# A list scheduler given deadlines and measured durations, and a last norm that VectorE scales out of PSUM

## The chip, the cores and the metric

One NeuronCore of a Trainium2 chip runs the whole program. The metric is the device time of one execution in microseconds. Three executions of the kernel before were timed: 2470.39, 2470.67 and 2472.54 us, so its median is 2470.67 us. A fourth, profiled execution took 2468.28 us; all rows below come from that one.

## The reference, cut to what matters

A trunk of two layers works on x, 1024 tokens by 1024 channels, in float32. Each layer has a token mixer and a gated ConvFFN, and a final RMSNorm closes the trunk.

```python
for i in range(DEPTH):                     # DEPTH = 2
    h = rms_norm(x, norm_g[i, 0]) * (1.0 + sc1) + sh1
    y = spatial_gating_mixer(h, ...) if i % 2 == 0 else hgrn2_mixer(h, ...)
    x = x + g1 * y
    h = rms_norm(x, norm_g[i, 1]) * (1.0 + sc2) + sh2
    x = x + g2 * conv_ffn(h, ...)          # (gelu(conv(gate)) * conv(val)) @ w_down
return rms_norm(x, final_g)                # x * rsqrt(mean(x*x) + eps) * g
```

The shifts, scales and gates sh, sc, g are six slices of `silu(c) @ ada_w[i] + ada_b[i]`. The first mixer (gMLP) projects to 4096 columns, normalises half of them, mixes tokens in blocks of 128 per head and multiplies by the other half. The second (HGRN2) is a gated linear recurrence with eight heads, chunked along the tokens.

## The kernel before, in words

The residual x lives in SBUF transposed, as the tile `xT`: 128 partitions, 8 channel groups d, 1024 tokens, worked on in two halves of 512. Each large product is made on TensorE from operands that are split into a high and a low part: three matmuls (high by high, high by low, low by high) are summed in one PSUM bank by `mm3` (L247). So every weight and every activation needs a split ahead of its matmuls: ScalarE makes the high part (L445), and VectorE or GpSimd the low part by a subtraction (L448; `n`, `w`, `h` and `raw` are the buffers that it writes). The large products are further done two blocks at a time with seven partial products for eight (`Pairs`), which costs VectorE sums of operands (`p_comb`, L455) and, out of PSUM, ScalarE copies (`snap`, L673) and VectorE sums of the results (`add`, L676).

The norms: ScalarE squares a piece (L399), the squares are summed over the eight groups by VectorE (L404), TensorE sums over partitions (L308), a chain of ten small VectorE instructions takes the reciprocal root (L281 to L291), VectorE writes it to a diagonal (L313), TensorE broadcasts it to all partitions (L318), and ScalarE copies it from PSUM to SBUF (L322). Then x is scaled (L970 in the first norm, L1667 in the last) and, before a mixer, split again by `p_h` (ScalarE L432, VectorE L433). The conditioning is made on VectorE by dot products with ada_w, one pair of 128x1024 operands each (`p_dot`, L255); there are 81 of them, spread over the first layer's work.

No engine's order is written out by hand. The kernel records some 8,300 operations in a class `Plan` as (engine, duration, function, predecessors, hand-given priority, port), where predecessors follow from the parts of tiles read and written. `emit` (L162 to L203) then plays them through a list scheduler: at each step it takes the ready operation that could start earliest on its engine by the durations given, and at equal starts the one with the lower hand-given number. Operations marked `port` (most VectorE work with two SBUF inputs, and GpSimd's) exclude each other in that plan. The instructions are issued on each engine in the order of the planned starts, and on the chip each engine runs them in that order, waiting for semaphores.

Places named later: `done` (L1210) multiplies the two halves of the gMLP in SBUF and PSUM; `entry` (L1228) scales a piece of x for the gMLP's second projection; `shifted` (L621) makes an operand of the seven products; `p_evac` (L387) adds a finished PSUM bank to `xT`; `lv_mm`, `adv` and `adv_t` (L1462 to L1490) are the recurrence's levels. At the end, `f1_last` takes the last two quarters of 256 tokens: groups d = 4 to 7 of both are done earlier, and d = 0 to 3 come last. `p_final` (L1667) scales `xT` by the broadcast root and issues a store (L1669) at once; the final gain is put on ahead of it by ScalarE (`p_gain`, L1674).

Of the kernel before, what the change touches and what calls it, by code (L numbers as in the profile page):

```python
# [98 lines left out]

class Plan:  # L100
# [9 lines left out]
    LOAD = 2.0  # L110

# [50 lines left out]
    def emit(self):  # L162
        n = len(self.ops)
        left = [0] * n
        users = [[] for _ in range(n)]
        for i, o in enumerate(self.ops):
            for q in set(o[3]):
                users[q].append(i)
                left[i] += 1
# [7 lines left out]
        while len(order) < n:  # L177
            best = None
            for eng, lst in ready.items():
                f = free.get(eng, 0.0)  # L180
                for i in lst:
                    o = self.ops[i]
# [4 lines left out]
            eng, dur, fn, _, _, pt = self.ops[i]  # L187
# [6 lines left out]
            for u in users[i]:  # L194
                e2 = self.ops[u][0]
                lat = self.LOAD if eng == "D" else self.LAT if e2 != eng else self.CHAIN if eng == "V" else 0.0
                est[u] = max(est[u], end[i] + lat)
                left[u] -= 1
                if not left[u]:
                    ready.setdefault(e2, []).append(u)  # L200
        for _, _, i in sorted(order):
            self.ops[i][2]()
        return max(end)  # L203
# [10 lines left out]
def trunk(tc, a, pool, psum, dram):  # L214
# [168 lines left out]
    def p_evac(pl, ps, d, hs, gate, which, pr):  # L383
# [5 lines left out]
        return pl.op("V", 0.15 + 0.6 * w, fn, r=(ps, x, modrg(*which, d)), w=(x,), pr=pr)  # L389

    def p_sum(pl, nm, d, accv, sqs, pr, eng="V", first=0):
# [15 lines left out]
    def p_stats(pl, nm, accv, ps, rbv, pr, part=0):  # L407
# [8 lines left out]
        pl.op("V", 1.3, chain, r=(ps,), w=(sm,), pr=pr)  # L416
# [4 lines left out]
    def p_t(pl, nm, l, sub, d, tv, rbv, pr):  # L421
        i = (l * 2 + sub) * KT + d
        return pl.op("V", 0.67, lambda: V.scalar_tensor_tensor(out=tv.f, in0=xT[:, d, nm.hs],
# [18 lines left out]
    def p_split(pl, src, hi, lo, eng, pr, *preds):  # L442
# [4 lines left out]
        return pl.op(eng, (0.1 + 0.53 * w) if eng == "V" else 0.1 + 1.17 * w,  # L447
# [131 lines left out]
    class Pairs:  # L579
# [32 lines left out]
        def combos(self, k, pr, t1=None):  # L612
# [7 lines left out]
            def shifted(out, x, s, y, srg, pr):  # L620
                pl.op("V", 0.67, lambda: V.scalar_tensor_tensor(out=out.f, in0=x.f, scalar=s, in1=y.f,  # L621
# [26 lines left out]
        def pair(self, j, fine=False):  # L648
# [26 lines left out]
            def add(c, ps, i):  # L675
                pl.op("V", 0.75, lambda: V.tensor_tensor(out=c.f, in0=ps.f, in1=c.f, op=ALU.add), r=(ps, c),  # L676
# [1112 lines left out]
```

## Time and profile before

| | |
|---|---|
| timed executions (us) | 2470.39, 2470.67, 2472.54 |
| profiled execution (us) | 2468.28 |
| span of its profile (us) | 2466.5 |
| PE busy | 2419.2 us, 98% of the span |
| DVE busy | 1992.3 us, 81% |
| ACT busy | 1205.9 us, 49% |
| POOL busy | 487.2 us, 20% |
| mean granted TensorE clock | 0.993 |

The profiled execution has 1.78 us outside its span and lies 2.39 us under the median. PE is TensorE's matmuls, DVE is VectorE, ACT is ScalarE, POOL is GpSimd, SP the engine that issues the transfers. The rows of the trace further down have the source line behind an L; a tile's buffer number is left out of its name, so `w<-w,w` reads two buffers of one family and writes a third.

### The profile page before, as it was taken

What the parts mean: (1) busy time and instruction counts of PE and PEld (TensorE: products, weight loads), DVE (VectorE), ACT (ScalarE), POOL (GpSimd) and SP (SyncE); (2) the same over time, 40 slices, a digit from 0 to 9 for tenths busy, and PEclk for the clock granted to TensorE, in tenths of its full rate; (3) what the DMA queues carried; (4) which work ended last, traced back from release to release, by engine and by line L of the source; (5) the groups of instructions that cost most, each with busy time, mean ns of one, the idle gap of its engine ahead of it and who ended that gap; (6) DMA issues with size and microseconds to landing.
All of it is one profiled execution on the core that took longest, in us unless ns stands there. A gap on an engine that the chain in (4) does not pass through costs nothing.

```text
span 2466.5 us, 33569 instructions
## 1 busy us (share of the span) xinstructions
PE 2419.2 (98%) x11850; PEld 2024.6 (82%) x11850; DVE 1992.3 (81%) x3179; ACT 1205.9 (49%) x2067; POOL 487.2 (20%) x294
## 2 busy tenths in 40 slices
PE   9999999999999999999999999999999999999997
PEld 7878777788788888888899898888777888888886
DVE  8989987988998888967746666658998998889766
ACT  5324654455555554445544444435454555554544
POOL 0232211122222221013321111100312222220122
PEclk9999999999999999999999999999999999999998
DMA  9997678621333324734110111123302332238332
GB/s 356 305 344 272 200 238 295 222 77 39 116 102 108 116 94 143 262 112 120 51 48 35 58 42 56 44 73 106 106 24 95 98 132 99 94 127 283 95 116 81
DMA packets 156411, 332.00 MB, mean 135 GB/s; under 512 B 15825, under 2 KB 34641, under 8 KB 156242
## 3 DMA queue, kind: packets, MB, share of 16 engines
q1 hardware_dynamic: 156242, 329.86, 40.0%
q8 instruction: 93, 1.52, 0.3%
q14 instruction: 76, 0.62, 0.1%
HBM read 254.82 MB, written 74.97 MB: 134 GB/s over the span
## 4 chain that ended last, share of the span: by engine, by line
PE 76%; DVE 8%; DMA 3%; ACT 2%; issue 1%; SPq 0%; DVEq 0%; ACTq 0%
PE pb L247 69%; PE pb L1462 3%; DMA n<-in_wo 1%; DMA xT<-vd 1%; DMA n<-in_down 1%; DVE h L448 1%; ACT xT L1171 1%; PE pb L1531 1%; PE pb L1551 1%; DVE w L448 1%; DVE raw L831 1%; PE pb L1553 1%; DVE n L448 0%; DVE xT L455 0%; DVE w L455 0%
## 5 line engine op out<-in xcount | busy, mean ns | idle before, releaser
L247 PE MATMUL pb<-h,w 128*128 128x512 f32 (+1 forms) x4212 | 981.7, 389 | 12.8 <-DVE h L448 4.1
L247 PE MATMUL pb<-n,w 128*128 128x512 f32 x3936 | 951.6, 394 | 6.8 <-ACT wk L673 4.4
L247 PEld LDWEIGHTS pb<-h,w 128*128 128x128 f32 x4212 | 785.5, 188 | 185.0 <-DVE h L448 9.6
L247 PEld LDWEIGHTS pb<-n,w 128*128 128x128 f32 x3936 | 731.9, 188 | 160.0 <-ACT wk L673 5.5
L448 POOL TENSOR_TENSOR w<-w,w 128x512 fp32r<-128x512 f32 x158 | 252.2, 1604 | 862.5 <-ACT w L445 784.2
L445 ACT ACTIVATE w<-w 128x512 fp32r<-128x512 f32 x384 | 237.3, 626 | 212.4 <-PE pb L247 121.7
L247 PE MATMUL pb<-w,n 128*128 128x512 f32 (+1 forms) x1536 | 273.6, 338 | 3.0 <-POOL w L448 1.7
L247 PEld LDWEIGHTS pb<-w,n 128*128 128x128 f32 x1536 | 237.9, 190 | 36.3 <-POOL w L448 2.1
L831 DVE SCALAR_TENSOR_TENSOR raw<-wk,prm,raw 128x1024 f32<-128x1024 f32 x168 | 251.7, 1520 | 16.2 <-ACT raw L827 14.1
L448 POOL TENSOR_TENSOR w<-raw,w 128x1024 fp32r<-128x1024 f32 (+1 forms) x48 | 118.3, 2473 | 536.0 <-ACT w L445 467.0
L448 DVE TENSOR_TENSOR w<-w,w 128x512 fp32r<-128x512 f32 x226 | 166.4, 741 | 41.5 <-ACT w L445 41.4
L673 ACT ACTIVATE wk<-pb 128x512 f32<-128x512 f32 x160 | 95.2, 599 | 174.5 <-PE pb L247 161.9
L445 ACT ACTIVATE w<-n 128x512 fp32r<-128x512 f32 x136 | 85.7, 630 | 158.0 <-PE pb L247 143.7
L676 DVE TENSOR_TENSOR wk<-pb,wk 128x512 f32<-128x512 f32 x160 | 109.2, 687 | 50.1 <-PE pb L247 30.9
L448 DVE TENSOR_TENSOR w<-n,w 128x512 fp32r<-128x512 f32 x136 | 103.4, 763 | 56.5 <-ACT w L445 56.4
L445 ACT ACTIVATE h<-h 128x512 fp32r<-128x512 f32 x198 | 122.3, 619 | 40.8 <-DMA h<-gact 23.5
L827 ACT ACTIVATE raw<-wk,prm 128x1024 f32<-128x1024 f32 x84 | 104.2, 1243 | 41.6 <-DVE wk L676 34.9
L448 POOL TENSOR_TENSOR h<-h,h 128x512 fp32r<-128x512 f32 x48 | 67.8, 1413 | 258.8 <-ACT h L445 247.4
L1468 DVE TENSOR_TENSOR wk<-wk 128x256 f32<-128x256 f32 x192 | 95.6, 523 | 23.7 <-PE pb L1462 11.0
L255 DVE SCALAR_TENSOR_TENSOR h<-h,raw 128x1024 f32<-128x1024 f32 x81 | 111.1, 1404 | 3.5 <-DMA h<-in_ada 3.4
L448 DVE TENSOR_TENSOR h<-h,h 128x512 fp32r<-128x512 f32 x150 | 102.1, 686 | 8.7 <-ACT h L445 8.7
L1472 ACT ACTIVATE wk<-wk 128x256 f32<-128x256 f32 x192 | 73.9, 415 | 59.4 <-PE pb L1462 44.2
(217 smaller groups left out, 2431.8 us busy)
## 6 DMA issues: line engine op xcount, KB each, us to landing
w<-in_up SPq DMA_DIRECT2D x88, 512.0 KB, 3.5
h<-in_ada SPq DMA_DIRECT2D x81, 512.0 KB, 6.3
act<-raw SPq DMA_DIRECT2D x154, 256.0 KB, 2.0
h<-act SPq DMA_DIRECT2D x124, 256.0 KB, 2.7
n<-in_down SPq DMA_DIRECT2D x64, 256.0 KB, 5.3
h<-gact SPq DMA_DIRECT2D x56, 256.0 KB, 2.7
gact<-xT SPq DMA_DIRECT2D x52, 256.0 KB, 3.9
vd<-h SPq DMA_DIRECT2D x32, 256.0 KB, 5.1
```

The source lines that it names most:

```text
L247: PE.matmul(ps, L[i // 2], R[i % 2], start=first and i == 0 and not more, stop=last and i == 2, skip_group_check=more)
L255: V.scalar_tensor_tensor(out=raw, in0=raw, scalar=1.0, in1=condr, op0=ALU.mult, op1=ALU.mult, accum_out=mod[:, m:m + 1])
L445: pl.op("S", 0.2 + 0.43 * w, lambda: S.activation(hi.r, src.f, AF.Copy), r=(src,), w=(hi,), pr=pr)
L448: lambda: e.tensor_tensor(out=lo.r, in0=src.f, in1=hi.f, op=ALU.subtract), *preds,
L673: pl.op("S", 0.6, lambda: S.activation(c.f, ps.f, AF.Copy), r=(ps,), w=(c,), pr=p(i) - 10)
L676: pl.op("V", 0.75, lambda: V.tensor_tensor(out=c.f, in0=ps.f, in1=c.f, op=ALU.add), r=(ps, c), w=(c,), pr=p(i) - 8)
L827: pl.op("S", 1.15, lambda: S.activation(y.f, wk[:, o + PADW:o + PADW + T], AF.Identity, bias=pc("conv_b", l * NUP + b), scale=cw(2)), r=(c ...
L831: pl.op("V", 1.17, lambda w=w: V.scalar_tensor_tensor(out=y.f, in0=wk[:, o + w:o + w + T], scalar=cw(w), in1=y.f, op0=ALU.mult, op1=ALU.ad ...
L1171: S.activation(x, x, AF.Identity, scale=lnr[:, tb:tb + 1], bias=nmr[:, tb:tb + 1])
L1462: PE.matmul(ps_()[0:m, c, :], K.f[:, c * P:c * P + m], q, start=True, stop=True)
L1468: V.tensor_tensor(out=halves_(X2, s)[:, :, i, :], in0=halves_(X, s)[:, :, i, :], in1=pair2()[:, :, o].unsqueeze(2).to_broadcast([P, 256 // ...
L1472: S.activation(halves_(X2, s)[:, :, i, :], halves_(X, s)[:, :, i, :], AF.Copy)
```

## The change

It has two parts. First, the planner runs twice. Its first pass goes by the hand-given numbers as before; TensorE's order is taken from it. From that order, with the durations given, each operation gets a latest start: the position in time of the TensorE work that needs it, less the durations and lags in between. The second pass is the same list scheduler, with these latest starts in the place of the hand-given numbers (for TensorE its position in the first pass; for what no TensorE work needs, the end of all TensorE work). Some thirty durations given to `pl.op` are replaced by others that stand nearer to the rows of the trace.

Second, the last norm: in `f1_last` the squares of the last pieces are no longer added up by VectorE but summed by TensorE in PSUM (`p_root`), the broadcast root stays in PSUM, and VectorE scales from there; GpSimd keeps five pieces of the first quarter, three of them held until the second chain of small instructions is through, and scales them by a copy that ScalarE makes. Stores are separate operations (`p_store`), six instead of fifteen.

```diff
+    def schedule(self, users, rank):
...
-                    t = max(f, est[i], port if o[5] else 0.0)
-                    if best is None or (t, o[4], i) < best:
-                        best = (t, o[4], i)
+                    t = max(f, est[i], port if self.ops[i][5] else 0.0)
+                    if best is None or (t, rank[i], i) < best:
+                        best = (t, rank[i], i)
...
+    def emit(self):
...
+        order = self.schedule(users, [o[4] for o in self.ops])
+        for _ in range(self.ROUNDS):
+            on_pe = [i for i in order if self.ops[i][0] == "PE"]
+            late, t = [FAR] * n, 0.0
+            for i in on_pe:
+                late[i] = t
+                t += self.ops[i][1]
+            for i in reversed(order):
+                for u in users[i]:
+                    late[i] = min(late[i], late[u] - self.lag(i, u) - self.ops[i][1])
+            rank = [min(x, t) for x in late]
+            for k, i in enumerate(on_pe):
+                rank[i] = k
+            order = self.schedule(users, rank)
+        for i in order:
             self.ops[i][2]()
...
-        pl.op("V", 1.3, chain, r=(ps,), w=(sm,), pr=pr)
+        pl.op("V", 1.95, chain, r=(ps,), w=(sm,), pr=pr)
...
-        return pl.op(eng, (0.1 + 0.53 * w) if eng == "V" else 0.1 + 1.17 * w,
+        return pl.op(eng, (0.11 + 0.57 * w) if eng == "V" else 0.1 + 1.22 * w,
...
-        pl.op("V", 2.2, fn, r=(kv(96 * hf, 96),), w=((f"small{hf}", 0, 16), kv(3264 + 8 * hf, 8), kv(3280 + 4 * hf, 4),
+        pl.op("V", 3.3, fn, r=(kv(96 * hf, 96),), w=((f"small{hf}", 0, 16), kv(3264 + 8 * hf, 8), kv(3280 + 4 * hf, 4),
...
+    def p_root(nm, sums, ps, pr, part):
+        c_, sm, accv = nm.n // P, (f"small{part}", 0, 16), sums[0]
+        nm.acc = accv.f
+        for i, x in enumerate(sums):
+            def fn(i=i, x=x):
+                for c in range(c_):
+                    PE.matmul(ps.f[:, c:c + 1], x.f[:, c * P:(c + 1) * P], ones[:, 0:1], start=i == 0 and c == 0,
+                              stop=i == len(sums) - 1, skip_group_check=True)
+            pl.op("PE", 0.23 * c_, fn, r=(x,), w=(ps,), pr=pr)
...
     def f1_last(mm, at):
...
+        _, b0 = p_root(nms[1], (accv[1], tails[3]), bv(4), at() - 4, 0)
+        for d in range(4):
             piece(1, d)
+        pl.op("S", 0.4, lambda: nms[1].copy_rb(bank[4][:, 0:256], rbv[1].f), b0, w=(rbv[1],), pr=at() - 4)
+        for d in (7, 0):
+            p_final(nms[1], d, 1, rbv[1], "G", at() - 3, b0)
+        for d in (4, 5):
+            p_final(nms[1], d, 1, bv(4, 0, 256), "V", at() - 2, b0)
+        p_store(nms[1], 4, 2, at())
+        c1, b1 = p_root(nms[2], (accv[2], *(tails[4 + d] for d in range(4))), bv(5), at() - 4, 1)
+        for d in (1, 2, 3):
+            p_final(nms[1], d, 1, rbv[1], "G", at(), b0, c1)
+        p_final(nms[1], 6, 1, bv(4, 0, 256), "V", at() - 1, b0, c1)
+        p_store(nms[1], 6, 2, at())
+        for d in range(0, KT, 2):
+            p_final(nms[2], d, 2, bv(5, 0, 256), "V", at() + 1, b1)
```

All lines of the file behind `emit` stand 25 lines lower after the change (L448 is L473 there, L455 is L480, L1210 is L1235, L1228 is L1253, L255 is L280, L433 is L458, L970 is L995, L387 is L412).

At three places VectorE's order is shown as it stands before and after. The first is the start, from the second dot product to the first low half. `h11` is the first norm's scratch, `n100` the low half of the first piece of the activations, `w1`, `w3` and `w5` low halves of weights. Before:

```order
L970 SCALAR_TENSOR_TENSOR h11_186<-xT_64,amul_71,pb6_81 128x512
L448 TENSOR_TENSOR w1_196<-h2_133,w0_167 128x1024
L448 TENSOR_TENSOR w3_202<-h3_145,w2_176 128x1024
L433 SCALAR_TENSOR_TENSOR n100_207<-h11_186,mod_70,n000_200 128x512
L255 SCALAR_TENSOR_TENSOR h4_162,mod_70<-h4_162,raw2_67 128x1024
L255 SCALAR_TENSOR_TENSOR h5_172,mod_70<-h5_172,raw2_67 128x1024
L263 TENSOR_TENSOR mod_70<-mod_70,prm_63 128x2
L267 SCALAR_TENSOR_TENSOR amul_71<-mod_70,prm_63 128x1
L970 SCALAR_TENSOR_TENSOR h11_186<-xT_64,amul_71,h10_198 128x512
```

After:

```order
L995 SCALAR_TENSOR_TENSOR h11_187<-xT_64,amul_71,pb6_81 128x512
L473 TENSOR_TENSOR w3_199<-h3_133,w2_165 128x1024
L473 TENSOR_TENSOR w1_204<-h2_141,w0_175 128x1024
L280 SCALAR_TENSOR_TENSOR h4_161,mod_70<-h4_161,raw2_67 128x1024
L280 SCALAR_TENSOR_TENSOR h5_171,mod_70<-h5_171,raw2_67 128x1024
L288 TENSOR_TENSOR mod_70<-mod_70,prm_63 128x2
L292 SCALAR_TENSOR_TENSOR amul_71<-mod_70,prm_63 128x1
L995 SCALAR_TENSOR_TENSOR h11_187<-xT_64,amul_71,h10_206 128x512
L458 SCALAR_TENSOR_TENSOR n100_208<-h11_187,mod_70,n000_202 128x512
```

The low half `n100` moved from ahead of the next two dot products and the second piece's scaling to behind them.

The second place is in the gMLP, where two `done` products (`xT<-pb5`) release the next spatial mixing on TensorE. Before:

```order
L448 TENSOR_TENSOR w3_1389<-w10_1550,w3_1389 128x512
L1228 SCALAR_TENSOR_TENSOR raw0_65<-raw0_65,amul_71,h10_198 128x512 x2
L1228 SCALAR_TENSOR_TENSOR raw1_66<-raw1_66,amul_71,h10_198 128x512
L1199 SCALAR_TENSOR_TENSOR pb5_80<-pb5_80,prm_63,wk_68 128x512
L1199 SCALAR_TENSOR_TENSOR pb4_79<-pb4_79,prm_63,wk_68 128x512
...
L455 TENSOR_TENSOR xT_64<-raw1_66,raw0_65 128x512
L455 TENSOR_TENSOR w10_1550<-w10_1550 128x512
L621 SCALAR_TENSOR_TENSOR raw1_66<-raw1_66,small_73 128x512
L1210 TENSOR_TENSOR xT_64<-pb5_80,xT_64 128x512
```

After:

```order
L473 TENSOR_TENSOR w3_1382<-w10_1491,w3_1382 128x512
L480 TENSOR_TENSOR h4_1857<-xT_64 128x512
L1253 SCALAR_TENSOR_TENSOR raw0_65<-raw0_65,amul_71,h10_206 128x512
L1224 SCALAR_TENSOR_TENSOR pb5_80<-pb5_80,prm_63,wk_68 128x512
L1224 SCALAR_TENSOR_TENSOR pb4_79<-pb4_79,prm_63,wk_68 128x512
L1235 TENSOR_TENSOR xT_64<-pb5_80,xT_64 128x512
L1253 SCALAR_TENSOR_TENSOR raw1_66<-raw1_66,amul_71,h10_206 128x512 x2
L480 TENSOR_TENSOR xT_64<-raw1_66,raw0_65 128x512
L280 SCALAR_TENSOR_TENSOR h3_133,mod_70<-h3_133,raw2_67 128x1024
L646 SCALAR_TENSOR_TENSOR raw1_66<-raw1_66,small_73 128x512
```

Three of the four `entry` scalings, a sum of operands and a `shifted` moved from ahead of the product to behind it. Over the whole queue sixteen operations that stood ahead of it now stand behind (the others are dot products, low halves and sums further up), and none the other way.

The third place is VectorE's end. Before:

```order
L387 SCALAR_TENSOR_TENSOR xT_64<-pb3_78,mod_70,xT_64 128x256
L404 TENSOR_TENSOR h1_16829<-h1_16829,h8_16846 128x256 x2
L281 TENSOR_SCALAR small_73<-pb1_76 128x2
...
L291 SCALAR_TENSOR_TENSOR small_73<-small_73 128x2
L313 TENSOR_TENSOR h1_16829<-prm_63,small_73 128x256
L1667 TENSOR_TENSOR xT_64<-xT_64,h9_17519 128x256 x4
L1667 TENSOR_TENSOR xT_64<-xT_64,h9_17519 128x2x256
```

After:

```order
L412 SCALAR_TENSOR_TENSOR xT_64<-pb3_78,mod_70,xT_64 128x256
L1692 TENSOR_TENSOR xT_64<-xT_64,pb4_79 128x256 x2
L306 TENSOR_SCALAR small_73<-pb5_80 128x2
...
L316 SCALAR_TENSOR_TENSOR small_73<-small_73 128x2
L338 TENSOR_TENSOR h1_87<-prm_63,small_73 128x256
L1692 TENSOR_TENSOR xT_64<-xT_64,pb4_79 128x256
L1692 TENSOR_TENSOR xT_64<-xT_64,pb5_80 128x2x256 x4
```

The additions of squares (L404) are gone from ahead of the last chain, two scalings out of PSUM stand in their place, and five scalings follow it as before, of which four instead of one are twice as wide.

## Rows read from the trace of the kernel before

**Rows 1.** Busy time by stretch: start:end, length, five engines, PEclk, DMA share, GB/s.
```profile
60.00:1050.00 990.00, 972.49 (x4376) 800.45 (x4375) 881.43 (x1255) 493.72 (x821) 211.56 (x125) 1.00 0.54 183
1050.00:1700.00 650.00, 648.64 (x3908) 569.23 (x3907) 413.94 (x927) 293.79 (x586) 114.99 (x58) 1.00 0.20 64
1700.00:1900.00 200.00, 189.99 (x862) 153.62 (x861) 182.97 (x288) 103.25 (x174) 49.22 (x28) 0.98 0.25 82
1900.00:2440.00 540.00, 539.59 (x2382) 445.17 (x2381) 446.73 (x576) 277.32 (x432) 103.64 (x69) 1.00 0.40 128
2440.00:2466.50 26.50, 11.43 (x80) 10.01 (x78) 16.78 (x45) 7.36 (x18) 7.58 (x10) 0.71 0.24 80
```

**Rows 2.** What TensorE waited for, 60 to 2440 us: total us, times, longest.
```profile
PE pb L247 <- ACT wk L673: 4.8, 3, 3.8
PE pb L247 <- ACT xT L673: 4.6, 4, 1.6
...
PE pb L247 <- DVE n L448: 2.9, 1, 2.9
...
PE pb L1194 <- ACT h L445: 2.4, 1, 2.4
PE pb L247 <- ACT h L445: 2.2, 2, 2.1
PE pb L247 <- POOL w L448: 1.7, 1, 1.7
PE pb L318 <- DVE h L313: 1.6, 4, 0.4
PE pb L1524 <- DVE wk L1468: 0.9, 1, 0.9
```

**Rows 3.** Busy time by stretch, behind four of these waits; PEclk is third from last.
```profile
263.35:266.76 3.41, 3.41 (x14) 2.93 (x13) 3.41 (x7) 3.15 (x7) 0.89 (x1) 0.50 0.42 129
...
403.30:406.71 3.41, 3.41 (x8) 2.73 (x9) 3.01 (x5) 2.33 (x5) 1.29 (x1) 0.50 0.98 285
...
1874.44:1881.27 6.83, 6.19 (x15) 4.84 (x16) 3.76 (x6) 1.08 (x3) 1.27 (x1) 0.50 0.31 115
...
1739.00:1742.40 3.40, 3.40 (x15) 2.78 (x16) 3.40 (x6) 0.77 (x2) 0.00 (x0) 1.00 0.63 160
```

**Rows 4.** GpSimd's low halves, a group of the page's part 5: busy us, mean ns.
```profile
L448 POOL TENSOR_TENSOR w<-w,w 128x512 fp32r<-128x512 f32 x158 | 252.2, 1604 | 862.5 <-ACT w L445 784.2
```

**Rows 5.** Timeline of the start, 20 to 28 us: start, duration, engine, operation.
```profile
21.39 5.75 PE L247 MATMUL pb<-w,n 128*128 128x512 f32 x24 [0.93 <-ACT n L432]
22.28 0.75 DVE L433 SCALAR_TENSOR_TENSOR n<-h,mod,n 128x512 fp32r<-128x512 f32 x1
22.94 1.22 DVE L255 SCALAR_TENSOR_TENSOR h<-h,raw 128x1024 f32<-128x1024 f32 x1
...
26.41 1.22 DVE L448 TENSOR_TENSOR w<-h,w 128x1024 fp32r<-128x1024 f32 x1
...
27.31 0.98 PE L247 MATMUL pb<-w,n 128*128 128x512 f32 x3 [0.17 <-ACT n L432]
```

**Rows 6.** Timeline of the end, 2448 to 2466 us, in order of start.
```profile
2450.85 5.75 POOL L1667 TENSOR_TENSOR xT<-xT,h 128x256 f32<-128x256 f32 x8 [17.26 <-ACT h L322]
...
2451.61 12.13 SPq L1669 DMA_DIRECT2D out_y<-xT  x15
...
2453.24 0.67 DVE L282 TENSOR_SCALAR small<-small 128x2 int32<-128x2 int32 x1
...
2456.66 0.16 DVE L288 SCALAR_TENSOR_TENSOR small<-small 128x2 f32<-128x2 f32 x1
...
2459.18 0.38 ACT L322 ACTIVATE h<-pb 128x256 f32<-128x256 f32 x1 [7.16 <-PE pb L318]
2459.59 3.09 DVE L1667 TENSOR_TENSOR xT<-xT,h 128x256 f32<-128x256 f32 x5 [1.73 <-ACT h L322]
```

**Rows 7.** Transfers of 2440 to 2467 us: size of one, median us to landing.
```profile
out_y<-xT SPq DMA_DIRECT2D x14, 128.0 KB, 1.7
out_y<-xT SPq DMA_DIRECT2D x1, 256.0 KB, 2.2
```

**Rows 8.** GpSimd's timeline, 265 to 272 us.
```profile
265.88 6.83 POOL L448 TENSOR_TENSOR w<-w,w 128x512 fp32r<-128x512 f32 x2 [8.82 <-ACT w L445]
```

**Rows 9.** Busy time by stretch, as in rows 1, around the wait at 263 us.
```profile
246.00:308.00 62.00, 57.60 (x285) 48.28 (x284) 59.21 (x93) 43.25 (x93) 13.97 (x7) 0.97 0.61 200
```

More of the change, by code (lines that the diff above doesn't have):

```diff
@@ L110 @@
     LOAD = 2.0
+    ROUNDS = 1
     def __init__(self):
@@ L160, in op, with lag @@
         return i
-    def emit(self):
+    def lag(self, i, u):
+        eng, e2 = self.ops[i][0], self.ops[u][0]
+        return self.LOAD if eng == "D" else self.LAT if e2 != eng else self.CHAIN if eng == "V" else 0.0
+    def schedule(self, users, rank):
         n = len(self.ops)
[L164 to L169, printed above, removed]
+        left = [len(o[3]) for o in self.ops]
         est, end = [0.0] * n, [0.0] * n
@@ L194, in emit @@
             for u in users[i]:
-                e2 = self.ops[u][0]
-                lat = self.LOAD if eng == "D" else self.LAT if e2 != eng else self.CHAIN if eng == "V" else 0.0
-                est[u] = max(est[u], end[i] + lat)
+                est[u] = max(est[u], end[i] + self.lag(i, u))
                 left[u] -= 1
                 if not left[u]:
-                    ready.setdefault(e2, []).append(u)
-        for _, _, i in sorted(order):
+                    ready.setdefault(self.ops[u][0], []).append(u)
+        return [i for _, _, i in sorted(order)]
+    def emit(self):
+        n = len(self.ops)
+        users = [[] for _ in range(n)]
+        for i, o in enumerate(self.ops):
+            for q in o[3]:
+                users[q].append(i)
+        order = self.schedule(users, [o[4] for o in self.ops])
[13 more added lines that the diff above has]
+        for i in order:
             self.ops[i][2]()
-        return max(end)
 def trunk_body(tc, a):
@@ L1665, in p_final, with p_store @@
         xr = [xrg(d + i, nm.hs) for i in range(k)]
[L1666 to L1669 removed]
+        pl.op(eng, (0.11 + 0.57 * w) if eng == "V" else 0.1 + 1.22 * w,
+              lambda: e.tensor_tensor(out=x, in0=x, in1=rb.f[:, 0:nm.n].unsqueeze(1).to_broadcast([P, k, nm.n]), op=ALU.mult),
+              *preds, r=(*xr, *((rb,) if eng == "G" or not preds else ())), w=xr, pr=pr, port=eng == "G" or not preds)
+    def p_store(nm, d, k, pr):
+        x = xT[:, d:d + k, nm.hs]
+        pl.op("D", 0.3 + 0.73 * k * nm.n / 512, lambda: nc.sync.dma_start(a["out"][:, d:d + k, nm.hs], x),
+              r=[xrg(d + i, nm.hs) for i in range(k)], pr=pr)
     def p_gain(nm, d, pr):
@@ L1675, in p_gain, with chain @@
               w=(xr,), pr=pr)
+    def p_root(nm, sums, ps, pr, part):
[7 more added lines that the diff above has]
+            pl.op("PE", 0.23 * c_, fn, r=(x,), w=(ps,), pr=pr)
+        rt, ops = small_ops(ps.f[:, 0:c_], c_, 1.0 / D, part)
+        def chain():
+            for f in ops:
+                f()
+        last = pl.op("V", 1.95, chain, r=(ps,), w=(sm,), pr=pr)
+        pl.op("V", 0.42, lambda: nm.diag(rt), r=(sm,), w=(accv,), pr=pr)
+        return last, pl.op("PE", 0.45, lambda: nm.bcast(ps.f[:, 0:nm.n]), r=(accv,), w=(ps,), pr=pr)
     def f1_first(pr):
@@ L1691, in piece @@
         def piece(i, d):
-            p_evac(pl, mm(d, 256 * i, 256), d, nms[1 + i].hs, gate2(1), (1, 5), at() - 4)
-            summed(i, d)
-        def finish(i, engs):
-            p_stats(pl, nms[1 + i], accv[1 + i], bv(i), rbv[1 + i], at() - 4, i)
-            d = 0
-            for e in engs.split():
-                k = int(e[1:])
-                p_final(nms[1 + i], d, k, rbv[1 + i], e[0], at() + d)
-                d += k
+            nm = nms[1 + i]
+            p_evac(pl, mm(d, 256 * i, 256), d, nm.hs, gate2(1), (1, 5), at() - 4)
+            if i == 0 and d < 3:
+                summed(i, d)
+            else:
+                x, q = xrg(d, nm.hs), tails[4 * i + d]
+                pl.op("S", 0.42, lambda: S.activation(q.f, xT[:, d, nm.hs], AF.Square), r=(x,), w=(q,), pr=at() - 4)
+            p_gain(nm, d, at() - 3)
+        last = two(f1.bc[11], F32)[0].life
+        tails = {3: View(acl, 0, 256), **{4 + d: View(last, 256 * d, 256) for d in range(4)}}
         for d in range(4, KT):
```

60 lines of the change are left out of this document (27 added, 33 removed).

## The prediction

> **What bounds the kernel now.** TensorE. I read first the busy time by stretch. From 60 to 2440 us its idle time is 990 - 972.49, plus 1.36, 10.01 and 0.41, together 29.3 us [rows 1]: nearly all of it lies in the first layer up to 1050 us and in the 200 us after the recurrence, the stretches in which VectorE is busy for 89 and 91% of the time. In the recurrence and in the second ConvFFN there is next to nothing to win. Next the waits by releaser: single waits of 1 to 4 us, which end with a ScalarE copy out of PSUM (9.4 us in seven), a VectorE low half, ScalarE high halves, and one GpSimd low half [rows 2]. Behind the longest of them the clock falls: three stretches of 3.41, 3.41 and 6.83 us stand at 0.50, that is 1.2 GHz for 2.4 GHz [rows 3]. TensorE worked in them for 3.41, 3.41 and 6.19 us and did half as much as at full clock, so they cost 1.7 + 1.7 + 3.1 = 6.5 us more. The waits of mid-run are thus worth 29.3 + 6.5 = 35.8 us. The last 26.5 us hold 11.43 us of TensorE work and a serial end [rows 1].
>
> **The mid-run waits.** The new tie-break changes no amount of work, only who goes first, so I costed each wait by VectorE's queue: the operations that stand ahead of the awaited one before and behind it after, less those that go the other way, by their durations in the trace. At the gMLP's wait (263 us, 2.4 us, ended on paper by a ScalarE high half, in fact by the `done` product ahead of it in the same chain) sixteen operations or 13.3 us go out and none comes in; the excerpt shows five of them. A wait can be paid back by that much, at most by its own length, so it goes, with its clock. By the same count 5.5 us go out ahead of the 2.9 us low half at 1739 us, 18 less 7 ahead of one at 432 us, and 2 to 10 us ahead of the ScalarE copies that release the seven products: those copies are short and wait themselves for VectorE's sums in the same bank chain. At the GpSimd wait of 1.7 us (163 us) 17 us go out of the chain behind it and 1.5 come in.
>
> Four do not go. The load of `h` at 402 us (2.06 us, a transfer queued behind as many bytes as before) keeps its wait and its low clock: 2.1 + 1.7 = 3.8 us. The recurrence's wait (0.9 us) has no work moved out ahead of it; a norm's broadcast at 1811 us (0.45 us) gets 0.7 to 1.4 us more ahead of it. At 1875 us only 2.5 us go out ahead of a 3.8 us wait, so 1.3 us stay, shorter than waits that left the clock alone. Together 6.5 us stay and 29.3 us go.
>
> **New waits.** The queue says where slack went. VectorE's low halves come 3 to 8 us earlier against their matmuls nearly everywhere. GpSimd's in the first ConvFFN come later: against 12 to 13.6 us before they keep 1 to 5 us, since work of no urgency now ranks behind and the first pair's products are pulled ahead by up to 16 us. At 281 us one stands 2.9 us behind its need. GpSimd's mean is 1.60 us [rows 4], so a margin of 1 us holds if nothing stretches it. I take 3 us, that one; the bounds are 0 and 6, with one such wait more.
>
> **The start.** The excerpt puts two dot products, two small operations and a scaling ahead of the first low half `n100`. They take from 22.94 to 26.41 us, 3.47 us [rows 5]. TensorE's first eight matmuls need no low half; the other sixteen of the 24 do. Those eight last 8/24 of 5.75 = 1.9 us, to about 23.3 us, while the low half was ready at 23.03, some 0.2 us ahead. So TensorE waits 3.3 us in mid-row, and falls back 2.9 us, since the two pauses just after (0.17 us and one of 0.2) are absorbed. What cover is there? None: all other products ahead need the same half. A 2.4 us wait lowered the clock, a 2.9 us one at 1739 us didn't [rows 3]; this one is longer and comes soon after the engine's start, so I add 1.7 us: 4.6 us. Bounds: 0 (if the dots wait less, or TensorE's later slack absorbs it) and 4.6. ScalarE's first high half moves ahead of a copy, which starts TensorE some 0.6 us earlier and gains nothing for the sixteen.
>
> Here a page bears. The Trainium skill ("TensorE: Matmul & The Clock Gate", Part 1: The HAM clock gate) says that the gate's default is the throttled state and activity releases it; it speaks against every order that leaves TensorE idle early. By it the start is 4.6 us, and without it 2.9; the row at 1739 us shows an idle engine that kept its clock, so the 1.7 us are not certain.
>
> **The end.** Before, half of the last chain of small instructions ran at 0.64 to 0.67 us for 0.16 beside GpSimd's eight scalings [rows 6], 2.4 us in five. After, two GpSimd scalings are ahead of the chain and three behind it, so most of that goes; I leave 1 us of it for the two. The ScalarE copy of 0.38 us goes from the path, and one addition of squares (0.4 us) too. Against that, the stores start later: nearly all of them after the chain, 1.5 MB of 2, where before eight had already gone out beside it. Fifteen stores of 128 KB take 1.7 us each to landing, overlapped, one of 256 KB 2.2 [rows 7]; the stretch's densest part ran at 200 to 290 GB/s, so 1.5 MB need 5.2 to 7.5 us. The scalings begin about 1.9 us earlier (2459.6 to 2457.7), and 1.5 MB from there land at 2463 to 2465.5, against 2465.5. I take -0.9 us; bounds -3.5 (transfers keep up) and +1 (they don't).
>
> The scalings out of PSUM have no row. The nearest is the same operation out of SBUF, five in 3.09 us beside two of GpSimd [rows 6]. The Trainium skill ("SBUF — State Buffer", Who interferes with whom) says that a VectorE instruction with at most one SBUF input, outside the two-port modes, doesn't contend with GpSimd: by it the PSUM scalings run free, some 0.5 us better than my sum. A row goes against reading it widely: L282 has one tile as input and took 0.67 us beside GpSimd [rows 6].
>
> **The sum.** -29.3 (waits and clock) + 3 (new waits) + 4.6 (start) - 0.9 (end) = -22.6 us. On the profiled execution that is 2468.28 - 22.6 = 2445.7; the median is 2.39 us above it, so I predict 2448.0 us.
>
> **The rivals.** *All goes* (0.08): the transfer's wait goes too, no new wait, the clock at the start holds: -35.8 + 2.9 - 0.9 = -33.8, 2437 us. For it: VectorE's slack grows almost everywhere. Against: the transfer has as many bytes ahead.
>
> *ScalarE's waits stay* (0.16): the waits that end with ScalarE are ScalarE's own lateness, not VectorE's: 4.8 + 4.6 + 2.4 + 2.2 = 14.0 us and all the low clock of 6.5, of which 5.1 are in the sum already, 15.4 more: 2463 us. For it: the trace names ScalarE. Against: ScalarE is busy half the time, and in each of these chains a VectorE step stands just before.
>
> *GpSimd late* (0.09), the other sign: its low halves are needed within 1 to 5 us now, and beside VectorE they can stretch: two took 6.83 us where 3.2 are usual [rows 8], 3.6 us late. With 1 us of margin that is 2.6 us of wait, in each of the 13 product pairs of the first layer 34 us, and the change ends at 2448 + 34 = 2482 us. It is slower from (22.6 + 4.9)/13 = 2.1 us a pair on. For it: VectorE is busy for 59.2 of 62 us there [rows 9]. Against: most of the 158 are near the mean.
>
> *The order matters little* (0.05): at 59.2 of 62 us busy VectorE may only hand the lateness on from one operation to the next, and 20 us return in new places: 2468 us.
>
> **The numbers.** The forecast itself has 0.62. A measurement of this kernel tells 0.2%, 4.9 us, from no change. Faster by more: the forecast, all goes, and ScalarE's waits (7.7 us below) make 0.86, less 0.03 for the latter's spread: 0.83. Within: 0.08. Slower: 0.09. The range takes the forecast with its bounds (new waits -3 to +3, start down to 0, end -2.6 to +1.9, two or three waits more or less) and both cases on the fast side: 2436 to 2464 us.
>
> **What would show it.** The profile after should have TensorE's idle time from 60 to 2440 us near 8 us (6.5 less the clock's 1.7, plus 3), no wait at 263 and 1739 us, a clock of 1.00 there; a wait of about 3.3 us in mid-row near 22 us, on VectorE's `n100`; a last chain near 0.2 us a step; and the last store landing about 1 us sooner after TensorE's last product. It is wrong if a GpSimd low half is the commonest releaser, if the waits on ScalarE's copies stay at 9 us, or if VectorE's busy time grows by more than the few us that its changed ends explain.

## The result and the profile after

The changed kernel takes 2452.29 us (median of four, 2449.32 to 2455.03) where the kernel before took 2470.53 beside it. The ratio is 0.9936 with a 95% interval of 0.9923 to 0.9950: 15.8 us faster by it, 12 to 19 by the interval; the medians lie 18.2 us apart. Forecast were 2448.0 us and 22.6 us less, range 2436 to 2464. The profiled execution took 2449.32 us, 19.0 us under the one of before; the terms are compared on these two.

Busy time by stretch in the changed kernel, which answers to [rows 1] (the start is added, the end left out):

```profile
0.00:60.00 60.00, 54.68 (x245) 45.99 (x246) 51.13 (x95) 30.14 (x40) 0.20 (x4) 0.94 0.95 358
60.00:1050.00 990.00, 980.50 (x4434) 809.84 (x4434) 878.24 (x1264) 497.79 (x834) 200.66 (x125) 1.00 0.55 185
1050.00:1700.00 650.00, 649.25 (x3919) 569.91 (x3918) 418.89 (x937) 292.15 (x586) 115.81 (x60) 1.00 0.21 64
1700.00:1900.00 200.00, 191.19 (x869) 155.06 (x868) 185.95 (x279) 103.92 (x171) 52.51 (x29) 0.99 0.26 82
```

TensorE idles for 9.5 us from 60 to 1050 where it was 17.5, but still for 8.8 us from 1700 to 1900 where it was 10.0: most of the gain lies in the first layer. What it waits for, 60 to 2430 us (us in total, times, longest), answers to [rows 2]:

```profile
PE pb L272 <- DVE n L473: 5.5, 5, 2.1
PE pb L272 <- ACT wk L698: 2.9, 3, 1.0
PE pb L272 <- DVE h L473: 2.5, 6, 0.9
PE pb L272 <- DVE xT L412: 1.9, 3, 1.5
PE pb L272 <- ACT xT L698: 1.7, 1, 1.7
PE pb L272 <- ACT n L457: 1.5, 1, 1.5
...
PE pb L272 <- ACT h L470: 0.7, 1, 0.7
```

All rows of that view make 18.7 us, for 29.2 before (by busy time TensorE idles for 19.1 us, for 29.3). The waits that ScalarE ends fell from 14 to 6.8 us, VectorE's low halves took first place, and no wait ends with GpSimd. The clock is at 0.50 in one stretch of mid-run (1846.63 to 1850.04 us), not three.

To see where the time went, I counted TensorE's matmuls in both traces and compared the end of the k-th: the changed kernel's end less that of before, at the time of before.

| at, us | 27 | 60 | 160 | 165 | 265 | 400 | 440 | 600 | 1700 | 1865 | 1900 | 2430 | end |
|---|---|---|---|---|---|---|---|---|---|---|---|---|---|
| lag, us | +2.5 | +1.5 | +1.2 | -0.7 | -4.0 | -5.2 | -11.2 | -12.3 | -11.9 | -10.0 | -15.6 | -17.1 | -19.0 |

The start costs 1.5 us, mid-run gives 18.6 back (13.4 to 1700 us, 5.2 behind), the end 1.9. Behind 1700 us new waits stand in the place of old ones; these rows are TensorE's (timelines of the changed kernel):

```profile
1734.33 3.01 PE L272 MATMUL pb<-n,n 128*128 128x512 f32 x12 [2.13 <-DVE n L473]
...
1805.40 0.51 PE L272 MATMUL pb<-n,w 128*128 128x512 f32 x1 [1.52 <-ACT n L457]
1806.63 1.66 PE L272 MATMUL pb<-n,w 128*128 128x512 f32 x6 [0.72 <-DVE n L458]
...
1844.97 0.96 PE L272 MATMUL pb<-n,w 128*128 128x512 f32 x3 [1.40 <-DVE n L473]
1846.83 1.22 PE L272 MATMUL pb<-n,w 128*128 128x512 f32 x2 [0.90 <-DVE n L473]
```

The start in the changed kernel (timeline: start, duration, engine, operation), which answers to [rows 5]:

```profile
20.14 2.14 PE L272 MATMUL pb<-w,n 128*128 128x512 f32 x8 [0.28 <-ACT n L457]
21.34 1.22 DVE L280 SCALAR_TENSOR_TENSOR h<-h,raw 128x1024 f32<-128x1024 f32 x1
22.48 1.22 DVE L280 SCALAR_TENSOR_TENSOR h<-h,raw 128x1024 f32<-128x1024 f32 x1
24.89 0.75 DVE L458 SCALAR_TENSOR_TENSOR n<-h,mod,n 128x512 fp32r<-128x512 f32 x1
25.69 2.57 PE L272 MATMUL pb<-w,n 128*128 128x512 f32 x10 [3.42 <-DVE n L458]
```

Eight matmuls run, then TensorE waits 3.42 us for the low half behind the two dot products: 3.3 was forecast. The end, which answers to [rows 6]:

```profile
2434.88 0.16 DVE L309 TENSOR_TENSOR small<-small 128x2 f32<-128x2 f32 x1
2435.01 3.44 POOL L1692 TENSOR_TENSOR xT<-xT,h 128x256 f32<-128x256 f32 x5 [18.79 <-ACT h L347]
2435.07 0.67 DVE L310 TENSOR_TENSOR small<-small 128x2 f32<-128x2 f32 x1
...
2438.50 0.16 DVE L315 TENSOR_TENSOR small<-small 128x2 f32<-128x2 f32 x1
...
2439.37 1.22 PE L343 MATMUL pb<-h,ones 128*128 128x256 f32 x2 [4.92 <-DVE h L338]
2439.71 4.27 SPq L1697 DMA_DIRECT2D out_y<-xT  x5
2440.63 2.48 DVE L1692 TENSOR_TENSOR xT<-xT,pb 128x512 f32<-128x512 f32 x4 [0.98 <-PE pb L343]
```

GpSimd's five scalings run in one piece beside the chain, and five of its steps take 0.64 to 0.67 us as before. The three that "wait for the chain" do so only in the plan: no data ties them to it, so on the chip GpSimd starts them as soon as their inputs are there.

### The profile page after: what moved, and what is told of

It is laid out like the page before. It is cut to its first block, busy times and chain, and to the rows that moved or that the text cites. A ratio compares the mean times of both kernels' runs of the same rounds, so it can differ in the third digit from the quotient of the medians.

```text
span 2447.5 us, 33499 instructions
## 1 busy us (share of the span) xinstructions
PE 2411.3 (99%) x11870; PEld 2025.4 (83%) x11870; DVE 1987.3 (81%) x3176; ACT 1199.3 (49%) x2066; POOL 473.3 (19%) x289
## 4 chain that ended last, share of the span: by engine, by line
PE 91%; DVE 4%; DMA 3%; ACT 1%; issue 1%; SPq 0%; DVEq 0%; ACTq 0%
PE pb L272 84%; PE pb L1487 3%; PE pb L1219 1%; DVE h L473 1%; PE pb L1556 1%; PE pb L1576 1%; PE pb L1578 0%; DMA xT<-vd 0%; DVE h L280 0%; PE pb L343 0%; DVE n L473 0%; DMA h<-in_ada 0%; DVE w L473 0%; PE pb L1549 0%; DMA w<-in_down 0%
## 5 line engine op out<-in xcount | busy, mean ns | idle before, releaser
L473 POOL TENSOR_TENSOR w<-w,w 128x512 fp32r<-128x512 f32 x158 | 249.6, 1586 | 862.6 <-ACT w L470 761.4
L856 DVE SCALAR_TENSOR_TENSOR raw<-wk,prm,raw 128x1024 f32<-128x1024 f32 x168 | 267.4, 1602 | 5.4 <-ACT raw L852 4.2
L473 POOL TENSOR_TENSOR w<-raw,w 128x1024 fp32r<-128x1024 f32 (+1 forms) x48 | 115.2, 2409 | 529.0 <-ACT w L470 450.5
L473 DVE TENSOR_TENSOR w<-w,w 128x512 fp32r<-128x512 f32 x226 | 161.2, 718 | 40.1 <-ACT w L470 39.4
L473 DVE TENSOR_TENSOR w<-n,w 128x512 fp32r<-128x512 f32 x136 | 100.8, 744 | 60.1 <-ACT w L470 59.7
L470 ACT ACTIVATE h<-h 128x512 fp32r<-128x512 f32 x198 | 122.1, 617 | 15.9 <-DVE h L473 5.8
L473 POOL TENSOR_TENSOR h<-h,h 128x512 fp32r<-128x512 f32 x48 | 67.9, 1416 | 256.0 <-ACT h L470 245.1
L473 DVE TENSOR_TENSOR h<-h,h 128x512 fp32r<-128x512 f32 x150 | 109.4, 732 | 5.0 <-ACT h L470 5.0
L280 DVE SCALAR_TENSOR_TENSOR h<-h,raw 128x1024 f32<-128x1024 f32 x81 | 103.5, 1305 | 1.5 <-DMA h<-in_ada 1.5
```

The source lines that it names most:

```text
L280: V.scalar_tensor_tensor(out=raw, in0=raw, scalar=1.0, in1=condr, op0=ALU.mult, op1=ALU.mult, accum_out=mod[:, m:m + 1])
L470: pl.op("S", 0.2 + 0.43 * w, lambda: S.activation(hi.r, src.f, AF.Copy), r=(src,), w=(hi,), pr=pr)
L473: lambda: e.tensor_tensor(out=lo.r, in0=src.f, in1=hi.f, op=ALU.subtract), *preds,
L856: pl.op("V", 1.26, lambda w=w: V.scalar_tensor_tensor(out=y.f, in0=wk[:, o + w:o + w + T], scalar=cw(w), in1=y.f, op0=ALU.mult, op1=ALU.ad ...
```

## The experiments

Two theories are told apart below. By A, TensorE is the bound and what it is spared stays won. By B, in the stretches where VectorE is busy for 90% and more, VectorE is the bound, and time won there comes back as a later wait.

One thing first, for every comparison of two traces below. Three kernels have one and the same order on TensorE, VectorE, ScalarE and GpSimd up to the last norm: the changed kernel, the new planner alone, and the end without GpSimd; a fourth, with one low half moved, has it up to 1730 us. Between 1800 and 1865 us the same six waits stand in all four, alike to 0.05 us. In the first layer they are not alike: at 364 us TensorE waits 1.72, 0.72, 1.43 and 0.70 us, and at 463 us 1.51 us, not at all, 1.51 us and not at all. The changed kernel's rows:

```profile
364.13 2.14 PE L272 MATMUL pb<-h,w 128*128 128x512 f32 x8 [1.72 <-ACT xT L698]
...
463.53 1.84 PE L272 MATMUL pb<-h,w 128*128 128x512 f32 x7 [1.51 <-DVE xT L412]
```

So between 60 and 1700 us a difference of 1 to 3 us between two single traces can be one of executions and not of kernels, and below I give what each of the four says.

**Which part carries it.** Four kernels. The first has the new planner and durations with the old last norm, the second the old planner with the new norm, the third the two passes with the old durations and the old norm, the fourth one pass with the new durations.

Each takes whole hunks of the change; of the durations, one stands for all:

```diff
-        pl.op("V", 1.3, chain, r=(ps,), w=(sm,), pr=pr)
+        pl.op("V", 1.95, chain, r=(ps,), w=(sm,), pr=pr)
...
```

> The new planner and its durations with the old last norm. Theory (the waits of mid-run go because VectorE's order changes): nearly all of the gain, about 17 us below the kernel before, TensorE idle from 60 us to the end region about 18 us as in the changed kernel, and the old end (last chain to last landing as before). Rival (the last norm carries the gain): within 3 us of the kernel before.

Measured: 2451.85 us, ratio 0.9934 (0.9919 to 0.9949). The planner alone has the whole gain. TensorE idles for 15.4 us from 60 to 2430 us, for about 18 expected.

> The old planner and its old durations with the new last norm. Theory: the middle as before (29 us of idle time), the end shorter by about 2 us, so 2468.5 where before has 2470.5. Rival (the norm carries the gain): 15 us or more below.

Measured: 2466.01 us beside 2468.92, ratio 0.9989 (0.9980 to 0.9999). The norm is worth 2.7 us by that ratio, 0.2 to 4.9. Beside the new planner it does not show: the kernel with both is not faster than the planner alone.

> Two passes with latest starts as ranks, but the old durations and the old last norm. Theory that the ranks carry the gain: at least 10 us below before. Rival that the measured durations carry it (a plan that is right about time needs no deadlines): under 5 us below.

Measured: 2451.07 us, ratio 0.9930 (0.9915 to 0.9944).

> One pass by the hand-given numbers, with the new durations and the old last norm. Theory that the ranks carry the gain: within 5 us of before. Rival that the durations carry it: 12 us or more below.

Measured: 2486.23 us, ratio 1.0071 (1.0055 to 1.0088): the durations alone make the kernel 17.5 us slower, which neither theory had. The ranks carry the whole gain, with either set of durations. The third kernel also shows whose order pays: up to 1700 us, by the names in the trace, 18 of its first 8,400 matmuls stand at another place than before, and yet 10.3 us are won there, so it is the order of the engines that feed TensorE that pays. The place differs, though: with the old durations 10.3 us are won to 1700 us and 10.9 behind, with the new ones (the first kernel) 17.7 and 2.9. Nothing that was tried here makes the totals agree.

The trace of the fourth kernel has 39.6 us of waits from 60 to 2430 us, four of them of 3.5 to 4.0 us (what TensorE waited for, 60 to 2430 us):

```profile
PE pb L247 <- DVE w L448: 9.4, 9, 3.6
PE pb L247 <- ACT wk L673: 9.4, 4, 4.0
PE pb L247 <- ACT h L445: 6.4, 2, 3.5
```

So durations nearer to the trace do not make a better order by themselves; why this one is worse, and which of the thirty durations does it, was not tried.

**The start.** One operation is moved in the finished order of the changed kernel: the low half `n100` (operation 71) ahead of the next two dot products (81).

```diff
+    MOVES = ((71, 81),)
...
+        for i, j in self.MOVES:
+            order.remove(i)
+            order.insert(order.index(j), i)
         for i in order:
             self.ops[i][2]()
```

> The changed kernel with one operation moved: the first low half (n100) ahead of the next two dot products on VectorE. Both theories: TensorE's 3.4 us wait at 22 us goes (under 0.5 us left), and it is 3 us ahead of the changed kernel at 60 us. Theory A (TensorE is the bound, time won early is kept): still 3 us ahead at 600 us and at the end, 2449 us where the changed kernel has 2452. Theory B (VectorE is the bound of the first layer, and it does not work sooner): the waits behind 160 us grow by as much, and at 600 us it is less than 1 us ahead.

Measured: 2446.27 us, ratio 0.9915 (0.9900 to 0.9930). TensorE's row at the start has no wait left in it:

```profile
20.09 6.10 PE L276 MATMUL pb<-w,n 128*128 128x512 f32 x24 [0.32 <-ACT n L461]
```

24 matmuls in one piece for 8 and a wait. Theory A holds for the start, by the times: 4.6 to 6.0 us less by the medians than the three kernels of the changed order that were timed four times, and its slowest execution is faster than their fastest. The traces alone would not settle it. Against the four kernels, in the order above, it is 2.0, 3.6, 5.6 and 4.6 us ahead at 60 us, 2.6, 0.6, 5.1 and 3.0 at 600, and 2.4, 2.0, 5.7 and 4.1 at 2300; A had 3 at 600, B under 1. Against the end without GpSimd (below) it is 5.6 and not 3.4 us because that execution began its first product 0.6 us later (20.66 for 20.09 us), and because of the clock. In the changed kernel's own profile the wait left it alone; in that other execution it fell (stretch, PE busy, ..., PEclk third from last; first the changed kernel, then the other):

```profile
25.69:32.50 6.81, 6.81 (x30) 5.64 (x31) 6.71 (x11) 2.77 (x4) 0.00 (x0) 1.00 1.02 402
```

```profile
25.71:32.54 6.83, 6.16 (x15) 4.80 (x16) 6.73 (x11) 3.46 (x4) 0.00 (x0) 0.50 0.99 335
```

At 0.50, 6.2 us of work hold 15 matmuls; at 1.00, 6.8 us hold 30. Seven of the profiled executions have this wait of 3.4 to 3.6 us at 26 us, and six of them a clock of 0.50 with it, for 6.8 us in five and 3.4 in one; the changed kernel's own is the exception.

**A wait put back.** In the changed kernel the gMLP product that releases TensorE at 260 us ends 5.7 us ahead of its matmul (253.98 and 259.68 us). Twelve VectorE operations were put back ahead of it.

```diff
+    MOVES = ((850, 915), (852, 915), (648, 915), (772, 915), (659, 915), (929, 915), (964, 915), (931, 915), (933, 915), (966, 915), (967, 915), (1053, 915))
```

> The changed kernel with twelve VectorE operations (9.4 us by their durations) put back ahead of the gMLP product that releases TensorE at 260 us. In the changed kernel that product ends 5.7 us ahead of its matmul. Theory (a wait is VectorE's queue ahead of the awaited operation): TensorE waits 9.4 - 5.7 = 3.7 us there, with a clock of 0.50 behind it. Rival (the awaited thing is ScalarE's or a transfer): no wait over 1 us. How much of it is left 60 us later, when the twelve no longer stand in the queue behind: theory A (TensorE is the bound) all of it, theory B (VectorE is) less than half.

Measured, on VectorE and on TensorE (timelines of that kernel):

```profile
266.56 0.68 DVE L1239 TENSOR_TENSOR xT<-pb,xT 128x512 f32<-128x512 f32 x1
```

```profile
267.34 1.24 PE L1223 MATMUL pb<-wk,xT 128*128 128x128 f32 x8 [3.73 <-issue]
```

The product ends at 267.24 us, the matmuls start 0.1 us later (the trace names no releaser, "issue"), and the wait is 3.73 us where 3.7 was forecast; the clock behind it is 0.50 for 3.4 us. So the count of VectorE's queue is right to the tenth for the wait that it is made for. What it does not tell is the rest. Wait and clock cost 5.6 us, against each of the four kernels with the changed order; 60 us later 3.0, 3.7, 3.4 and 2.8 of them are left, half to two thirds, where A had all and B less than half. The twelve stand no longer in the queue behind, and the waits just there shrink (2.4 us in four from 267 to 284 us in the changed kernel, 1.0 in two here). So part of it is handed back within 60 us, and neither theory has the size. What is left 200 us later cannot be read: 0.5, 4.0, 1.5 or 2.6 us, by the kernel that it is held against.

**A wait of ScalarE, and the port.** Two places in one kernel: ScalarE's copy out of PSUM (1320) ahead of four scalings (1352), and GpSimd's sum of squares (6029) ahead of its low half (5958).

```diff
+    MOVES = ((1320, 1352), (6029, 5958))
```

> The changed kernel with two operations moved at two places far apart. At 364 us ScalarE's copy out of PSUM goes ahead of a group of four scalings that waits for a transfer: if ScalarE's own order makes that wait, 1.7 us become under 0.3; if VectorE or the transfer does, nothing changes. At 1732 us a GpSimd sum of squares goes ahead of a GpSimd low half, so that it no longer runs beside the second of two VectorE low halves that took 1.6 and 1.8 us for 0.7: if the port that they share made the wait of 2.1 us there, it falls to about 1.1; if VectorE's queue did, it stays at 2.1.

Measured at 364 us, on TensorE:

```profile
362.20 2.98 PE L276 MATMUL pb<-n,w 128*128 128x512 f32 x12
365.02 2.88 PE L276 MATMUL pb<-h,w 128*128 128x512 f32 x12
```

The wait, 0.7 to 1.7 us in the four kernels, is gone: it was ScalarE's own order (its copy stood behind scalings that waited for a transfer), as the rival "ScalarE's waits stay" had it for this place. Whether the gain is kept this run does not tell. At 464 us it has a wait of 2.06 us for additions to the residual, with a low clock behind it, where two of the four wait 1.51 and two not at all; at 480 us, counted from 60 us, it is 1.0 us ahead of one of them, level with another, and 1.2 and 2.6 behind the others.

At 1734 us nothing changed (2.1 us): GpSimd's sum, moved ahead, took 7.65 us beside VectorE where it takes 1.3, and the low half behind it still met the two low halves of VectorE. So the collision came along, and the run tells nothing on the port. The next one took GpSimd's low half out.

```diff
-        e = V if eng == "V" else G
+        e = V if eng == "V" or len(pl.ops) == 5958 else G
```

> The changed kernel with one low half at 1730 us computed by VectorE in place of GpSimd, at its place in the plan's order (behind the two low halves that TensorE waits for at 1734 us). Moving a GpSimd sum there had changed nothing: the collision came along. Theory (the port that VectorE and GpSimd share makes that wait): the two low halves take 0.7 us again for 1.56 and 1.75, and the wait of 2.1 us falls under 0.4. Rival (VectorE's queue): it stays over 1.5.

VectorE's timeline there, in the changed kernel and in this one:

```profile
1731.04 1.56 DVE L473 TENSOR_TENSOR n<-n,n 128x512 fp32r<-128x512 f32 x1
1732.52 1.75 DVE L473 TENSOR_TENSOR n<-w,n 128x512 fp32r<-128x512 f32 x1
```

```profile
1730.91 1.58 DVE L473 TENSOR_TENSOR n<-n,n 128x512 fp32r<-128x512 f32 x1
1732.41 1.28 DVE L473 TENSOR_TENSOR n<-w,n 128x512 fp32r<-128x512 f32 x2
```

The second low half and the moved one now take 1.28 us together, and TensorE's wait falls from 2.13 to 1.08 us:

```profile
1733.15 5.05 PE L272 MATMUL pb<-n,n 128*128 128x512 f32 x21 [1.08 <-DVE n L473]
```

This difference is no scatter: the wait is 2.12 to 2.15 us in all seven traces with GpSimd's low half in this place, and 1.08 in both without it (the other is the kernel with all repairs, below). The first low half still takes 1.58 us, beside the GpSimd sum that drags on until 1731.9 us. Both expected numbers were missed; half the wait is shown to be the collision, and the other half is argued from that sum.

**The end.** GpSimd's five scalings and ScalarE's copy for them go to VectorE.

```diff
-        for d in (7, 0):
-            p_final(nms[1], d, 1, rbv[1], "G", at() - 3, b0)
...
-        for d in (1, 2, 3):
-            p_final(nms[1], d, 1, rbv[1], "G", at(), b0, c1)
...
+        for d in (6, 0, 2):
+            p_final(nms[1], d, 2, bv(4, 0, 256), "V", at() - 1, b0, c1)
```

> The changed kernel with the five scalings of GpSimd at the end, and ScalarE's copy for them, given to VectorE (two at a time, from PSUM, behind the last chain). Theory (GpSimd beside the chain makes its steps 0.65 us): the chain falls from 4.4 to 2.0 us, VectorE's added work of 2 us lies beside the broadcast and before the last scalings, and the last landing comes 1 to 2 us sooner after TensorE's last product. Rival (the stores' rate ends the kernel): the chain falls, the end stays within 0.5 us.

Timeline of its end:

```profile
2438.59 0.17 DVE L311 TENSOR_SCALAR small<-small 128x2 f32<-128x2 f32 x1
2440.12 4.26 DVE L1692 TENSOR_TENSOR xT<-xT,pb 128x512 f32<-128x512 f32 x7
2440.26 1.22 PE L343 MATMUL pb<-h,ones 128*128 128x256 f32 x2 [2.49 <-DVE h L338]
```

Every step of the chain is at 0.16 or 0.17, and TensorE's wait for it is 2.49 us for 4.92. From the last sums of TensorE to the end of the span it is 11.2 us where the changed kernel has 13.0: 1.8 us won. The median, 2450.82 us, lies within the scatter of the changed kernel.

**Together, and one more pass.**

```diff
+    MOVES = ((71, 81), (1320, 1352), (1448, 1771), (1451, 1771), (2348, 2295))
...
-    ROUNDS = 1
+    ROUNDS = 2
```

The first line is of the kernel with the repairs (with the end and the low half as above), the last two of the kernel with three passes (which has the start and the end mended too).

> The changed kernel with the first low half ahead of the dot products, the end without GpSimd, the low half of the run before on VectorE, and two repairs like that at 364 us: at 613 us ScalarE's copy out of PSUM ahead of a convolution, and at 461 us a dot product that waits for its load put behind the four additions to the residual that TensorE waits for. Start 3.4 us or, with the clock, up to 5.6; end 1.8; the four waits of mid-run 1.7 + 1.5 + 0.9 + 1.9 = 6 us. Theory A (TensorE is the bound, what is won stays): 2439 us where the changed kernel has 2452. Theory B (of what is won in the first layer's middle, most is given back in later waits on VectorE): 2444.

Measured: 2443.67 us, ratio to before 0.9900 (0.9885 to 0.9914), the lowest median here, faster than both kernels; the interval overlaps with that of the low half first alone. The median is theory B's; the profile is between the two: of the 6 us that were to go in mid-run, 3.9, 2.0, 3.7 and 3.1 are left at 2425 us by the count of matmuls against the four kernels. One place shows B beyond the scatter. At 613 us the repair won the wait of 0.86 us, and the next wait, 7 us on, grew from 1.03 to 1.80 (the first two rows are the changed kernel's, the third this one's):

```profile
613.18 1.21 PE L272 MATMUL pb<-h,w 128*128 128x512 f32 x4 [0.86 <-ACT wk L698]
625.42 0.96 PE L272 MATMUL pb<-n,w 128*128 128x512 f32 x3 [1.03 <-ACT wk L698]
...
620.27 3.03 PE L276 MATMUL pb<-n,w 128*128 128x512 f32 x12 [1.80 <-ACT wk L702]
```

The 1.03 us stand in all seven other traces of this planner's order, so 0.77 of 0.86 us were handed on. At 364 us 0.43 us of wait came back although the copy stands first here too, and the wait at 461 us, absent here, is absent in two traces without the repair as well.

> The changed kernel with one more pass of the scheduler (latest starts taken from the second pass), with the low half first at the start and the end without GpSimd. Theory that the ranks are what pays and a better order of TensorE's work gives better ranks: below 2442 us. Rival (one pass has what there is): within 3 us of the changed kernel less what the start and the end give, 2444.

Measured: 2447.25 us, ratio 0.9910 (0.9893 to 0.9926). One more pass gives nothing beyond the repairs of start and end: it is 3.3 us above the 2444 that these were to give, and the intervals of the three kernels with the start mended overlap.

## Why the prediction was right, and where not

**The direction and the mechanism** held: the waits of mid-run shrink because ranks by latest start put VectorE's unhurried work behind what TensorE waits for. The third and fourth kernels show that the ranks do it, the put-back shows the rule at one place to a tenth of a microsecond.

**"So it goes", said of the waits behind 1700 us, and "New waits",** are the steps that failed in size. The sum took 26.3 us out of mid-run (29.3 less 3); the count of matmuls has 18.6, and 20.6 and 18.8 in the two other kernels of the same order. Split at 1700 us, the forecast's terms are 14.6 us (with the 3 us of new waits taken off) and 11.8. Up to 1700 us 13.4, 17.7 and 15.9 were measured: that part held. Behind it 5.2, 2.9 and 2.9. Three things came out otherwise there. The wait at 1739 us, 2.9 us, was to go for good; 2.1 us of it stand at 1734, half of that shown to be two VectorE low halves beside GpSimd. Waits of 1.5 and 0.7 us stand at 1805 behind a norm's broadcast, for 0.7 and 0.45 before. And at 1845 us there are 1.4 and 0.9 us, with 3.4 us of low clock behind them in two of the three traces, for 0.5 and 0.7 before. I had looked for new waits on GpSimd alone, and these end with ScalarE and VectorE. They recur in every trace of this order, so they are the order's and not one execution's; the third kernel, with the old durations, has no wait at 1734 and 0.4 us at 1803, and wins 10.9 us behind 1700. Which of the new durations brought them is not known.

The rival "the order matters little" had lateness handed on in the first layer, where VectorE is busy for 59 of 62 us [rows 9]. There is some of it: the waits of 2.4, 0.7 and 1.3 us at 263, 276 and 297 us are 0.9, 0.4 and 0.9 us at 267, 273 and 284 us now, and the put-back and the repair at 613 us show it from the other side. But the first layer's sum came out without it.

**The waits said to go or stay.** At 432 us the wait went, and at 1875 us 1.0 us stayed of 3.8, for 1.3 forecast. At 402 us the load of `h` was to keep its wait "behind as many bytes": it is gone, without a low clock, and 0.2 and 0.5 us are left just behind. The load leaves SyncE's queue at 388.57 us for 395.39 before, 6.8 us sooner, where TensorE comes to it only 5.3 us sooner (395.1 for 400.5), and its split starts 5.9 us after the issue for 6.5. I had compared the bytes ahead of it, not the time of issue against TensorE's. At 364 us the wait stayed (1.7 us), ScalarE's own as the run shows; of the rival on ScalarE that much is true. Waits that ScalarE ends make 6.8 of its 14 us, but 1.5 of these are the new one at 1805.

**New waits.** No wait ended with GpSimd; the one at 281 us did not come, and "GpSimd late" fell. Its low halves did harm another way, by slowing VectorE beside them.

**The start** was right as a wait (3.42 us for 3.3). The profile has +1.5 us for the forecast 4.6: the first matmul came 1.25 us earlier, the lag fell from 2.5 to 1.5 us over the pauses behind, and the 1.7 us of low clock were missing in that execution. Over the seven executions with this start it is 1.5, 3.1, 4.0, 4.1, 5.0, 5.0 and 5.2 us at 60 us, so 4.6 was a fair size and the result's own profile the mild case; that it left the clock alone is luck. The low clock itself was mis-sized: 6.8 us of it in five of the six, up to 3.1 us for the 1.7, part of it absorbed behind. The sentence of the Trainium skill ("TensorE: Matmul & The Clock Gate", Part 1: The HAM clock gate) that spoke for the 1.7 us agrees with six executions of seven.

**The end** gave 1.9 us for 0.9, by errors that offset. The chain kept all of the 2.4 us that GpSimd costs it (I left 1, taking the plan's order for a wait on the chip). The copy's 0.4 us went as forecast: from TensorE's last sums to the first wide scaling it is 6.2 us for 6.6. The squares were worth more than the 0.4 us of one addition: from TensorE's last product to its last sums it is 1.7 us for 4.5, of which the sums that it now makes ahead of that product take 1.4 back. And the stores cost nothing, where I had them 1 us longer: from the first wide scaling to the end it is 6.9 us, as before, since they ran at 313 to 361 GB/s in slices of 0.3 us for the 200 to 290 assumed. (The items that I listed for the scalings' start, 1.4, 0.4 and 0.4, make 2.2 us and not 1.9.) The Trainium skill's rule on one SBUF input ("SBUF — State Buffer", Who interferes with whom) stays untested for the scalings out of PSUM: GpSimd was done (2438.45 us) before the four wide ones began (2440.63). The row on L282 does not go against it as I wrote: the rule leaves out the two-port modes, and L282 is a tensor_scalar, which the same section counts among the operations that can enter them; no row shows whether it did.

## What to carry to other kernels

A wait's cost can be read from the queue ahead of the awaited operation, in the put-back to the tenth; what its removal is worth cannot, where the engine that makes the operation is itself full. Add up such waits as a group, look for new ones on every engine and not on one, and expect part back at the next awaited operation (0.77 of 0.86 us at 613 us). Before reading a microsecond out of two traces, read two traces of one order: here single waits in the first layer differed by up to 1.5 us. Time spared at the start was mostly kept to the end. A list scheduler's predecessor that carries no data orders the plan and holds nothing on the chip, and a rank by latest start still lets it take, greedily, a 4 us operation that can start a moment sooner than the one TensorE waits for.

## What the runs showed of the hardware

A GpSimd sum of 128x512 that takes 1.29 us took 7.6 us beside a row of VectorE subtractions with two inputs in SBUF, in three kernels, and VectorE's own took 1.55 to 1.75 us for 0.69 where they met GpSimd's. The same start, with the same wait of 3.4 to 3.6 us, left TensorE's clock at 1.00 in one profiled execution and went with 0.50 in six. A chain of ten small VectorE steps took 0.64 to 0.67 us for each of the five that ran beside GpSimd, and 0.16 or 0.17 for all ten where GpSimd had nothing to do.
